# Turning the attention probabilities of 64-query halves by identity products on 64x64 parts, masking the first block like the others, and stepping chunk 2's mixing differently

## The chip, the core and the metric

The kernel runs on one core of a Trainium2 chip. The metric is the device time of one execution in microseconds (us); the kernel before is given by the median of three runs. The engines are TensorE (PE in the profile, its weight loads PEld), VectorE (DVE), ScalarE (ACT), GpSimd (POOL) and SyncE (SP), which issues most transfers (DMA).

## The reference, cut to what matters

One layer of a decoder trunk runs over 1,024 prompt tokens and 64 sample tokens: a SwiGLU block, a mixing layer, and a second SwiGLU block, each with a norm ahead and behind. The change lies in one half of the mixing layer, the sliding-window attention of the prompt. Eight query heads of 64 numbers share two key heads, a query sees the 128 positions before it and itself, and each head has a learned sink that takes part in the softmax's denominator:

```python
dist = qi + W - kj
band = (dist >= 0) & (dist <= WINDOW)
valid = (jnp.arange(nb)[:, None, None] > 0) | (kj >= W)[None]
s = jnp.where(band & valid, s, -jnp.inf)
m = jnp.maximum(jnp.max(s, -1, keepdims=True), sink)
p = jnp.exp(s - m)
p = p / (p.sum(-1, keepdims=True) + jnp.exp(sink - m))
out = jnp.einsum('bnhgqk,bnkhd->bnqhgd', p, vv)
```

The other half of the layer is a gated linear recurrence (HGRN2) in chunks. Everything is in float32.

## The kernel before, in words

**Chunks.** The 1,088 tokens are cut into three chunks: chunk 0 has 256 prompt tokens and the 64 sample tokens (320 wide), chunks 1 and 2 have 384 prompt tokens each. Nearly all the time goes to projections, in which each float32 operand is split into a rounded part and a remainder, and a product is made of three matmuls (lines 255 to 257, `mm3`). A weight tile comes by DMA (`raw`), ACT rounds it (line 235), DVE forms the remainder (line 236), and PE multiplies.

**Mixing beside projections.** What is not a projection is written as Python generators that stop at `yield`. A generator is registered as a stream with a rate. `tick()`, called once or twice for each weight tile, advances every stream by its rate, so mixing steps are dropped between projection products. `need(name)` runs the rest of a stream at once. The mixing streams are m0, m1 and m2, one for each chunk, with the rates `RM`. m0 runs beside the last part of the first SwiGLU block, m1 beside the output projection of chunk 0 and the input projection of chunk 2, m2 beside the output projection of chunk 1 and the first units of the second SwiGLU block (`f2.head`, whose cuts are `HEAD2`). In a mixing stream the recurrence (`intra`, then `hgrn_block`) and the attention (`attn_block`) take steps in turn. The framework then places each instruction on its engine by a planned timeline, so the order on an engine isn't quite that of the code. Each engine works its list in order.

**One attention block.** `attn_block(n, b)` works on 128 queries of chunk n, and does its eight heads in two rounds (`pr`) of four: two key heads `g`, two query heads `i`. A round has these steps:

- Scores, `sc`, line 1212: the 128 queries are two halves `hq` of 64. Each half needs 192 keys only, so the products are 64 queries by 192 keys, and the halves lie on the two halves of the partitions.
- Mask and maximum on DVE (line 1225), two tiny operations on the maxima (`sm`, lines 1228 and 1230), then the exponentials on ACT (line 1235), which write probabilities into the padded tile `pad` (512 wide, two heads of 192 with 64 columns at either end). POOL clears two corners of the pads (lines 1220 and 1221).
- After two yields the turning, `pT`, line 1248: PE's transpose takes windows of 64 queries by 128 keys and turns them, 16 of them in a round; a window may take in columns that are not wanted. One copy by DVE (`hq` 0) and one by ACT (`hq` 1) brings the turned tiles from PSUM to SBUF, 128x512 each (line 1253).
- After one more yield the product with the values, `pv`, line 1262: 12 products, each on 64 keys and 64 output columns, that take the four quarters of the PE array by turns. `PLACE` tells in which slot a half's key block `blk` stands. ACT and DVE copy and add the result (lines 1271 and 1272).

**The first block** of the prompt has no keys before it. There `cols_of` cuts the keys to 64 for the first half and 128 for the second, and mask and exponentials are done apart for each half: 8 of each in a round where other blocks have 4.

Names that the prediction uses besides: `lv` and `l` (lines 1316 and 1347) are products of the recurrence's `intra`; `av` (1403, 1406) those of its blocks; `pvT` (1280) the transposes of the attention's result; `tr` (452) transposes of the next SwiGLU block's or projection's input, for which line 444 scales rows by the root of `rsqrt`; `gb` (392) is a gain row that a DMA brings; `rb` (290) is a mean over partitions; `ar` is a piece of the SwiGLU activations that a DMA brings (993), rounded as `h`; `w` and `wsp` are weight tiles.

Of the kernel before, what the change touches and what calls it, by code (L numbers as in the profile page):

```python
# [8 lines left out]
F32 = mybir.dt.float32  # L9
# [4 lines left out]
AF = mybir.ActivationFunctionType  # L14
ALU = mybir.AluOpType
# [3 lines left out]
P = 128  # L19
# [11 lines left out]
NEG = -1e30  # L31
# [7 lines left out]
LEVELS = [64, 32, 16, 8, 4, 2, 1]  # L39
NRAW = 3  # L40
WARM = 12
PLACE = ((0, 0, 1), (1, 0, 0))
P1 = 1.0


# [1 line left out]
def tile_step(ctx: ExitStack, tc: tile.TileContext, A: dict, O: list):  # L47
    nc = tc.nc
    V, S, G, PE = nc.vector, nc.scalar, nc.gpsimd, nc.tensor
# [15 lines left out]
    def axbank(s="ax"):  # L65
        return ps.tile([P, 512], F32, tag="ax", bufs=4, name=uid(s))
# [53 lines left out]
    ident = cp.tile([P, P], F32, name="ident")  # L120
# [9 lines left out]
    halfpost = cp.tile([P, 16], F32, name="halfpost")  # L130
    sinkb = cp.tile([P, 8], F32, name="sinkb")
    amask = cp.tile([P, 192], F32, name="amask")
    smask = cp.tile([P, 136], F32, name="smask")
    ssink = cp.tile([P, 2], F32, name="ssink")
    seqm = cp.tile([NS, 4], F32, name="seqm")
# [10 lines left out]
    def mix_consts():  # L146
# [927 lines left out]
    def mixing(tp, h):  # L1074
        w_in, w_out = A["w_in"], A["w_out"][0]

        def t2(shape=(P, 512)):
            return tmp2("t2", shape)
# [21 lines left out]
        def w_in_units(n):  # L1100
# [88 lines left out]
        def attn_block(n, b):  # L1189
            zq, kx, vn = Z[n]["q"], KX[n], VN[n]  # L1190
            first = n == 0 and b == 0
            sm, mx = small(), small()
            of_ = t2()
            halves = (0, 1)

            def of(x, pr):
                return x.rearrange("p (g r i) -> p g r i", g=2, r=2)[:, :, pr]

            def cols_of(hq):
                return slice((128, 64)[hq] if first else 0, 192)  # L1200

            def rows(par):
                return slice(64 * par, 64 * par + 64)

            for pr in range(2):
                pt, banks = [], [axbank("sc")[:, :384].rearrange("p (i c) -> p i c", i=2) for _ in range(2)]
                for i in range(2):
                    for hq in halves:
                        cs = cols_of(hq)
                        k0 = b * P + 64 * hq  # L1210
                        for g in range(2):
                            PE.matmul(banks[g][rows(hq), i, cs],  # L1212
                                      zq[rows(g), 2 * pr + i, b * P + 64 * hq:b * P + 64 * hq + 64],
                                      kx[rows(g), k0 + cs.start:k0 + cs.stop], start=True, stop=True)
                parts = [(rows(hq), cols_of(hq)) for hq in halves] if first else [(slice(0, P), slice(0, 192))]
                for g in range(2):
                    pad = t2()
                    p = pad[:, 64:448].rearrange("p (i c) -> p i c", i=2)
                    pt.append((p, pad))
                    G.memset(pad[rows(0), 448:], 0.0)  # L1220
                    G.memset(pad[rows(1), :64], 0.0)
                    for i in range(2):
                        hd = 4 * g + 2 * pr + i
                        for rs, cs in parts:
                            V.tensor_tensor_reduce(out=p[rs, i, cs], in0=banks[g][rs, i, cs], in1=amask[rs, cs],
                                                   op0=ALU.add, op1=ALU.max, scale=1.0, scalar=NEG,
                                                   accum_out=mx[rs, 0, hd:hd + 1])
                V.scalar_tensor_tensor(of(sm[:, 0], pr), of(mx[:, 0], pr), 0.125, of(sinkb, pr),
                                       op0=ALU.mult, op1=ALU.max)
                V.tensor_scalar(of(sm[:, 1], pr), of(sm[:, 0], pr), -1.0, None, op0=ALU.mult)  # L1230
                for g in range(2):
                    for i in range(2):
                        hd = 4 * g + 2 * pr + i
                        for rs, cs in parts:
                            S.activation(pt[g][0][rs, i, cs], pt[g][0][rs, i, cs], AF.Exp, bias=sm[rs, 1, hd:hd + 1],  # L1235
                                         scale=0.125, accum_out=mx[rs, 1, hd:hd + 1])
                V.tensor_tensor(of(sm[:, 2], pr), of(sinkb, pr), of(sm[:, 0], pr), op=ALU.subtract)
                S.activation(of(sm[:, 2], pr), of(sm[:, 2], pr), AF.Exp)
                yield
                yield  # L1240
                pT, tb2 = [], [axbank("pT").rearrange("p (g i s q) -> p g i s q", g=2, i=2, s=2) for _ in range(2)]
                for g in range(2):
                    for i in range(2):
                        for slot, at in ((0, (0, 64)), (1, (128, -64))):
                            for hq in halves:
                                if not first or at[hq] >= cols_of(hq).start:
                                    c = 64 + 192 * i + at[hq]
                                    PE.transpose(tb2[hq][:, g, i, slot], pt[g][1][rows(hq), c:c + P],  # L1248
                                                 ident[rows(hq), rows(hq)])
                for hq in halves:  # L1250
                    t = t2((P, 2, 2, 2, 64))
                    ss = slice(1 - hq, 2 - hq) if first else slice(0, 2)
                    (S.copy if hq else V.tensor_copy)(t[:, :, :, ss], tb2[hq][:, :, :, ss])
# [3 lines left out]
                for turn in (((0, 0), (0, 1)), ((0, 2), (1, 0)), ((1, 1), (1, 2))):  # L1257
                    for g in range(2):
                        for par, (hq, blk) in enumerate(turn):
                            if 64 * blk >= cols_of(hq).start:  # L1260
                                alone = (hq, blk) in ((0, 1), (1, 1))
                                PE.matmul(ob[par][rows(g), :, hq], vn[rows(par), b + (blk + hq) // 2, rows(g)],  # L1262
                                          pT[hq][rows(par), g, :, PLACE[hq][blk]],
                                          start=alone or first or blk == 0, stop=alone or blk == 2)
                src = of_[:, pr * 256:pr * 256 + 256].rearrange("p (i h q) -> p i h q", i=2, h=2)
                if first:
                    S.copy(src[:, :, 0], ob[0][:, :, 0])
                    V.tensor_copy(src[:, :, 1], ob[0][:, :, 1])
                    V.tensor_tensor(src[:, :, 1], ob[1][:, :, 1], src[:, :, 1], op=ALU.add)
                else:  # L1270
                    S.copy(src, ob[0])
                    V.tensor_tensor(src, ob[1], src, op=ALU.add)
                if pr:
                    yield
            V.tensor_tensor(mx[:, 2], mx[:, 1], sm[:, 2], op=ALU.add)
            V.reciprocal(mx[:, 3], mx[:, 2])
            yield
            tb = axbank("pvT")
            for m in range(4):
                PE.transpose(tb[:, m * P:(m + 1) * P], of_[:, m * P:(m + 1) * P], ident)  # L1280
# [103 lines left out]
        def hgrn_block(n, b):  # L1384
# [458 lines left out]
```

## Time and profile before

| | |
|---|---|
| median of 3 runs | 1968.94 us (1964.67 to 1969.4) |
| the profiled execution: time, span | 1969.12 us, 1967.4 us |
| granted TensorE clock, mean | 0.996 |
| PE busy | 1942.1 us, 99% of the span |
| DVE busy | 1433.7 us, 73% |
| ACT busy | 949.6 us, 48% |
| POOL busy | 182.7 us, 9% |
| DMA, share of 16 engines on the hardware queue q1 | 54.4% |

Times in the profile are microseconds from the start of the span unless they are marked ns. A row of the timeline gives start, duration, engine, line, operation, the tiles written and read, the shape, and in square brackets the idle time before it and who ended that. `x24` is the number of records; a float32 product leaves two records (and two weight loads), a transpose or a product of rounded operands one. Such a row's duration goes from the first record's start to the last one's end. PEclk is the clock that the throttle granted to TensorE as a share of full speed.

### The profile page before, as it was taken

Reading aid. Unit: us, or ns where it says so; the run is one execution under the profiler, and the core shown is the slowest. Engines: PE = TensorE matmul, PEld = TensorE weight load, DVE = VectorE, ACT = ScalarE, POOL = GpSimd, SP = SyncE. Lnnn points to the kernel's source line nnn. Section 1 sums busy time; section 2 is a strip of 40 time slices with the busy share of each in tenths; the row PEclk is TensorE's granted clock in tenths of the full one; section 3 lists DMA queues with packets and bytes.
Section 4 is the critical chain, followed back from the end, with each engine's and each line's share of the span. In section 5 each row is a group of like instructions: output and inputs, shape, how many; then the busy total and the mean of one; then the engine's idle time right before and its main releaser. Section 6 shows DMA issues by size and latency. Waiting matters only on the chain.

```text
span 1967.4 us, 34910 instructions
## 1 busy us (share of the span) xinstructions
PE 1942.1 (99%) x13559; PEld 1817.4 (92%) x13559; DVE 1433.7 (73%) x2507; ACT 949.6 (48%) x1713; POOL 182.7 (9%) x225
## 2 busy tenths in 40 slices
PE   9999999999999999999999999999999999999998
PEld 9999999999998987778998898989999999999887
DVE  6896779886567646677577857866987877656666
ACT  5553445444445444445444545765544444445453
POOL 0300000000013102121031303000000000000202
PEclk9999999999999999999999999999999999999999
DMA  6643667655767546755434343536465545666974
GB/s 245 209 141 122 218 215 262 236 193 185 236 224 237 177 132 213 267 168 175 131 101 140 99 155 110 167 125 225 165 212 185 207 177 195 213 235 224 310 260 140
DMA packets 175606, 375.30 MB, mean 191 GB/s; under 512 B 16128, under 2 KB 67520, under 8 KB 175424
## 3 DMA queue, kind: packets, MB, share of 16 engines
q1 hardware_dynamic: 169536, 362.58, 54.4%
q10 hardware_dynamic: 5904, 10.49, 1.6%
q8 instruction: 106, 1.74, 0.3%
q14 instruction: 60, 0.49, 0.1%
HBM read 290.60 MB, written 83.39 MB: 190 GB/s over the span
## 4 chain that ended last, share of the span: by engine, by line
PE 88%; DMA 4%; DVE 4%; ACT 2%; issue 1%; POOL 0%; SPq 0%; ACTq 0%; DVEq 0%; POOLq 0%
PE mm L255 27%; PE mm L256 27%; PE mm L257 27%; DMA ar<-fa 1%; DMA raw<-in_ffn_w_gu_dram 1%; PE sc L1212 1%; ACT t L1235 1%; PE lv L1316 1%; DMA fb<-big 0%; PE pv L1262 0%; PE c L255 0%; PE c L257 0%; PE c L256 0%; DMA fa<-big 0%; PE pT L1248 0%
## 5 line engine op out<-in xcount | busy, mean ns | idle before, releaser
L255 PE MATMUL mm<-h,wsph 128*128 128x320 f32 (+1 forms) x1344 | 428.0, 319 | 0.0
L256 PE MATMUL mm<-h,wsph 128*128 128x320 f32 (+1 forms) x1344 | 425.2, 317 | 0.0
L257 PE MATMUL mm<-h,wspl 128*128 128x320 f32 (+1 forms) x1344 | 423.8, 317 | 0.0
L236 DVE TENSOR_TENSOR wspl<-raw,wsph 128x1024 fp32r<-128x1024 f32 x208 | 260.1, 1252 | 123.9 <-ACT wsph L235 123.1
L235 ACT CAST wsph<-raw 128x1024 fp32r<-128x1024 f32 x208 | 217.7, 1048 | 262.1 <-PE mm L256 211.0
L255 PEld LDWEIGHTS mm<-h,wsph 128*128 128x128 f32 x1344 | 252.8, 188 | 5.5 <-issue 3.8
L256 PEld LDWEIGHTS mm<-h,wsph 128*128 128x128 f32 x1344 | 252.9, 188 | 4.8 <-issue 4.0
L257 PEld LDWEIGHTS mm<-h,wspl 128*128 128x128 f32 x1344 | 252.4, 188 | 2.4 <-issue 2.1
L255 PE MATMUL mm<-h,w 128*128 128x384 f32 (+1 forms) x736 | 246.2, 334 | 3.0 <-ACT big L806 1.6
L256 PE MATMUL mm<-h,w 128*128 128x384 f32 (+1 forms) x736 | 245.5, 334 | 0.4 <-DVE h L617 0.3
L235 ACT CAST w<-raw 128x512 fp32r<-128x512 f32 (+1 forms) x208 | 153.5, 745 | 188.9 <-PE mm L256 93.5
L257 PE MATMUL mm<-h,w 128*128 128x384 f32 (+1 forms) x736 | 240.3, 333 | 0.5 <-POOL w L608 0.5
L236 DVE TENSOR_TENSOR w<-raw,w 128x512 fp32r<-128x512 f32 (+1 forms) x208 | 178.0, 862 | 75.6 <-ACT w L235 75.0
L256 PE MATMUL mm<-w,h 128*128 128x512 f32 x462 | 182.3, 395 | 0.9 <-DVE w L236 0.9
L255 PE MATMUL mm<-w,h 128*128 128x512 f32 x462 | 181.8, 396 | 0.7 <-DVE big L1006 0.7
L257 PE MATMUL mm<-w,h 128*128 128x512 f32 x462 | 180.8, 394 | 0.0
L256 PE MATMUL mm<-big,w 128*128 128x384 f32 x528 | 176.4, 334 | 0.0
L255 PE MATMUL mm<-big,w 128*128 128x384 f32 x528 | 176.4, 334 | 0.0
L257 PE MATMUL mm<-big,w 128*128 128x384 f32 x528 | 175.6, 334 | 0.0
L255 PEld LDWEIGHTS mm<-h,w 128*128 128x128 f32 x736 | 138.2, 188 | 4.8 <-ACT big L806 2.3
L256 PEld LDWEIGHTS mm<-h,w 128*128 128x128 f32 x736 | 138.2, 188 | 1.0 <-DVE h L617 0.8
L257 PEld LDWEIGHTS mm<-h,w 128*128 128x128 f32 x736 | 137.7, 188 | 1.1 <-POOL w L608 0.7
(346 smaller groups left out, 3379.8 us busy)
## 6 DMA issues: line engine op xcount, KB each, us to landing
raw<-in_ffn_w_gu_dram SPq DMA_DIRECT2D x162, 512.0 KB
raw<-in_ffn_w_down_dram SPq DMA_DIRECT2D x74, 512.0 KB
raw<-in_w_in_dram SPq DMA_DIRECT2D x54, 512.0 KB
ar<-fa SPq DMA_DIRECT2D x70, 384.0 KB
big<-in_ffn_w_down_dram SPq DMA_DIRECT2D x88, 256.0 KB
fb<-big SPq DMA_DIRECT2D x44, 512.0 KB
fa<-big SPq DMA_DIRECT2D x22, 768.0 KB
raw<-fb SPq DMA_DIRECT2D x30, 512.0 KB
```

What stands on the lines that cost most here:

```text
L235: made['S'] = S.copy(hi, src).ins
L236: (lo_eng or V).tensor_tensor(lo, src, hi.bitcast(F32), op=ALU.subtract)
L255: PE.matmul(out, a[0], b[0], start=first, stop=False, skip_group_check=resume)
L256: PE.matmul(out, a[0], b[1], start=False, stop=False, skip_group_check=resume)
L257: return PE.matmul(out, a[1], b[0], start=False, stop=last, skip_group_check=resume).ins
L1212: PE.matmul(banks[g][rows(hq), i, cs], zq[rows(g), 2 * pr + i, b * P + 64 * hq:b * P + 64 * hq + 64], kx[rows(g), k0 + cs.start:k0 + cs.st ...
L1235: S.activation(pt[g][0][rs, i, cs], pt[g][0][rs, i, cs], AF.Exp, bias=sm[rs, 1, hd:hd + 1], scale=0.125, accum_out=mx[rs, 1, hd:hd + 1])
L1316: PE.matmul(b5[32 * i:32 * i + 32, b, a], K[:, a, cs], Q[:, a, cs], start=True, stop=True)
```

## The change

The probabilities stand in a plain tile of 128 by 2 by 192. They are turned by 24 ordinary float32 products in a round, each of a 64x64 part with a 64x64 identity, where there were 16 transposes of 64x128 windows. Each part goes to the partitions on which the values' 64 rows stand, so a turned half fills one slot and half of another, and is copied in two pieces. The corners need no clearing. The first block uses the same 128 columns for both halves with a mask of its own (`amask1`), so mask and exponentials are done for all 128 partitions together. In chunk 2 there is one more yield ahead of `pv`; in chunks 1 and 2 one more ahead of a chunk's first `av`. The rates of m1 and m2 go from 0.92 and 1.2 to 1.08 and 1.30, and the first cut of `HEAD2` from 5 units to 4.

```diff
-PLACE = ((0, 0, 1), (1, 0, 0))
+TURNS = ((0, 0), (0, 1)), ((0, 2), (1, 0)), ((1, 1), (1, 2))
...
+        V.tensor_copy(amask1, amask[:, 64:192])
+        V.memset(amask1[0:64, 0:64], NEG)
...
-            if n:
+            if n == 0:
+                G.memset(kx[:, 64:P], 0.0)
+            else:
...
+            cs = slice(64 if first else 0, 192)
+            mask = amask1 if first else amask
+            pieces = [t for t in ((0, 0), (0, 1), (1, 1), (1, 0), (0, 2), (1, 2)) if not first or sum(t) > 1]
...
                 for g in range(2):
-                    pad = t2()
-                    p = pad[:, 64:448].rearrange("p (i c) -> p i c", i=2)
-                    pt.append((p, pad))
-                    G.memset(pad[rows(0), 448:], 0.0)
-                    G.memset(pad[rows(1), :64], 0.0)
+                    p = t2((P, 2, 192))
+                    pt.append(p)
                     for i in range(2):
                         hd = 4 * g + 2 * pr + i
-                        for rs, cs in parts:
-                            V.tensor_tensor_reduce(out=p[rs, i, cs], in0=banks[g][rs, i, cs], in1=amask[rs, cs],
...
+                        V.tensor_tensor_reduce(out=p[:, i, cs], in0=banks[g][:, i, cs], in1=mask,
...
-                        for rs, cs in parts:
-                            S.activation(pt[g][0][rs, i, cs], pt[g][0][rs, i, cs], AF.Exp, bias=sm[rs, 1, hd:hd + 1],
...
+                        S.activation(pt[g][:, i, cs], pt[g][:, i, cs], AF.Exp, bias=sm[:, 1, hd:hd + 1],
...
-                for g in range(2):
-                    for i in range(2):
-                        for slot, at in ((0, (0, 64)), (1, (128, -64))):
-                            for hq in halves:
-                                if not first or at[hq] >= cols_of(hq).start:
-                                    c = 64 + 192 * i + at[hq]
-                                    PE.transpose(tb2[hq][:, g, i, slot], pt[g][1][rows(hq), c:c + P],
-                                                 ident[rows(hq), rows(hq)])
+                for i in range(2):
+                    for g in range(2):
+                        for hq, blk in pieces:
+                            PE.matmul(tb2[hq][rows((hq + blk) % 2), g, i, blk // 2],
+                                      pt[g][rows(hq), i, 64 * blk:64 * blk + 64],
+                                      ident[rows(hq), rows(hq)], start=True, stop=True)
                 for hq in halves:
                     t = t2((P, 2, 2, 2, 64))
-                    ss = slice(1 - hq, 2 - hq) if first else slice(0, 2)
-                    (S.copy if hq else V.tensor_copy)(t[:, :, :, ss], tb2[hq][:, :, :, ss])
+                    copy = S.copy if hq else V.tensor_copy
...
+                        copy(t[:, :, :, 0], tb2[hq][:, :, :, 0])
+                        copy(t[rows(hq), :, :, 1], tb2[hq][rows(hq), :, :, 1])
                     pT.append(t)
                 yield
+                if n == 2:
+                    yield
...
             if b == 0:
                 yield
+                if n:
+                    yield
...
-    RM = [0.97, 0.92, 1.2]
+    RM = [0.97, 1.08, 1.30]
...
-    HEAD1, HEAD2 = 9, (5, 14, 22)
+    HEAD1, HEAD2 = 9, (4, 14, 22)
```

Because the timeline is planned anew, the order on the engines moves at many places of the mixing. Lines of the changed kernel lie some three to seven higher in number. Three places matter below. In the rows, numbers behind a name tell tiles of one kind apart, and only those within one kernel can be compared.

The first is DVE in the second round of the prompt's first block (chunk 0). Before, the last of the round's masked scores (the third and fourth of four 64-row operations on `t_1092`, the second bank) stand behind other work, and the tiny operations on the maxima (`sm_7301`), for which the exponentials wait, come after two operations of the recurrence (1331, 1355):

```order
L1225 ISA t_1092_7609,sm_7302<-sc_7593,amask 64x128
L1225 ISA sm_7302 64x1
L1331 COPY_PREDICATED cm_7214<-lm_88,lv_7628 128x256
L1355 TENSOR_TENSOR big_6792<-big_6792,big_7211 128x4x16x8
L1228 SCALAR_TENSOR_TENSOR sm_7301<-sm_7302,sinkb 128x2x2
L1230 TENSOR_SCALAR sm_7301<-sm_7301 128x2x2
L1237 TENSOR_TENSOR sm_7301<-sinkb,sm_7301 128x2x2
L236 TENSOR_TENSOR w_7853<-raw_7850,w_7852 128x1024
```

In the changed kernel:

```order
L1224 ISA t_1092_7602,sm_7306<-sc_7590,amask_84 128x128
L1224 ISA sm_7306 128x1
L1274 TENSOR_TENSOR t_1060_7307<-pv_7579,t_1060_7307 128x2x64
L1009 TENSOR_TENSOR big_6079<-mm_7179,big_6079 128x512
L1227 SCALAR_TENSOR_TENSOR sm_7305<-sm_7306,sinkb 128x2x2
L1009 TENSOR_TENSOR big_6079<-mm_7180,big_6079 128x512
L1229 TENSOR_SCALAR sm_7305<-sm_7305 128x2x2
L1235 TENSOR_TENSOR sm_7305<-sinkb,sm_7305 128x2x2
L239 TENSOR_TENSOR w_7790<-raw_7787,w_7789 128x1024
L1009 TENSOR_TENSOR big_6079<-mm_7181,big_6079 128x512
L239 TENSOR_TENSOR h_7961<-ar_7962,h_7961 128x2x384
```

The masks of the second bank and the three operations on the maxima now come ahead of the remainder of `w` (7790 is the same tile as 7800 before), behind which the second bank's masks stood, and ahead of the remainder of `h` (7961, before 7971). The recurrence's two operations (1336, 1360 in the new numbers) follow four rows further on.

The second is DVE where it makes the input of the second SwiGLU block's first transposes (`tr`, 452, read `big_5798`, which 444 writes). Before:

```order
L1272 TENSOR_TENSOR t_1159_8051<-pv_8440,t_1159_8051 128x256
L1380 TENSOR_TENSOR t_1230_8493<-hT_8488,big_7025 128x512
L224 SCALAR_TENSOR_TENSOR sm_8364<-sm_8364 128x3
L404 TENSOR_TENSOR big_7174<-big_7174,gb_8458 128x512
L1502 COPY t_1236_8539<-skT_8534 64x512
L1511 TENSOR_TENSOR t_1240_8546<-big_6922,seqm 64x512
L444 TENSOR_SCALAR big_5798<-big_5798,sm_8364 128x512 x3
```

In the changed kernel:

```order
L226 SCALAR_TENSOR_TENSOR sm_8356<-sm_8356 128x3
L1277 TENSOR_TENSOR t_1159_8041<-pv_8442,t_1159_8041 128x256
L227 SCALAR_TENSOR_TENSOR sm_8356<-sm_8356 128x3
L447 TENSOR_SCALAR big_5801<-big_5801,sm_8356 128x512 x2
L1385 TENSOR_TENSOR t_1230_8495<-hT_8490,big_7029 128x512
L447 TENSOR_SCALAR big_5801<-big_5801,sm_8356 128x512
L1174 TENSOR_TENSOR h_7214<-t_1230_8495,h_7212 128x4x128
L1509 COPY t_1236_8541<-skT_8536 64x512
L1518 TENSOR_TENSOR t_1240_8548<-big_6926,seqm 64x512
```

Two of the three scalings now stand ahead of the recurrence's operation (1380 before, 1385 now), and all three ahead of the sample tokens' (1502 and 1511, now 1509 and 1518).

The third is PE in the last round of chunk 0's attention, from the scores `sc` to the `pT` of the same round, for which mask, maxima and exponentials must be done in between. Before, 20 projection products of 512 columns stand there, beside the recurrence's eight `av` and four `u`:

```order
L1212 MATMUL sc_8225<-kx_6453,big_6520 64x192
L255 MATMUL mm_8410<-w_8311,h_8319 128x512
L256 MATMUL mm_8410<-w_8312,h_8319 128x512
L257 MATMUL mm_8410<-w_8311,h_8319 128x512
...
L1403 MATMUL av_8267<-big_6922,big_7212 128x128
L1406 MATMUL av_8267<-st,big_6792 128x128
...
L1410 MATMUL u_8339<-big_6922,t_1180_8178 128x128 x4
L256 MATMUL mm_8411<-w_8312,h_8319 128x512
...
L1248 MATMUL pT_8386<-ident,t_1189_8234 128x64
```

In the changed kernel ten do, and the `pT` follows right behind `u`:

```order
L1216 MATMUL sc_8221<-kx_6456,big_6524 64x192
L258 MATMUL mm_8011<-w_8177,h_8274 128x512
L259 MATMUL mm_8011<-w_8178,h_8274 128x512
L260 MATMUL mm_8011<-w_8177,h_8274 128x512
...
L1410 MATMUL av_8259<-big_6926,big_7216 128x128
L1413 MATMUL av_8259<-st,big_6796 128x128
...
L1417 MATMUL u_8331<-big_6926,t_1180_8174 128x128 x4
L1243 MATMUL pT_8378<-ident,t_1189_8230 64x64 x2
```

So the ten products that stood last between them have gone elsewhere. The same holds in the second round of chunk 1's second block, where 26 products of 384 columns, `av` and `u` lay between `sc` and `pT`, and now 15, `av` and four transposes (`kT`) do. Between `pT` and `pv`, under which the copies of the turned tiles run, there are at the end of chunk 2 twelve projection products in the last round and four in the round before it, where there were six and 25; in the other rounds nineteen instructions or more stand there before and after.

More of the change, by code (lines that the diff above doesn't have):

```diff
@@ L132, in tile_step @@
     amask = cp.tile([P, 192], F32, name="amask")
+    amask1 = cp.tile([P, P], F32, name="amask1")
     smask = cp.tile([P, 136], F32, name="smask")
@@ L1208, in attn_block @@
                     for hq in halves:
-                        cs = cols_of(hq)
                         k0 = b * P + 64 * hq
@@ L1214, in attn_block @@
                                       kx[rows(g), k0 + cs.start:k0 + cs.stop], start=True, stop=True)
-                parts = [(rows(hq), cols_of(hq)) for hq in halves] if first else [(slice(0, P), slice(0, 192))]
                 for g in range(2):
-                    pad = t2()
-                    p = pad[:, 64:448].rearrange("p (i c) -> p i c", i=2)
-                    pt.append((p, pad))
-                    G.memset(pad[rows(0), 448:], 0.0)
-                    G.memset(pad[rows(1), :64], 0.0)
+                    p = t2((P, 2, 192))
+                    pt.append(p)
                     for i in range(2):
                         hd = 4 * g + 2 * pr + i
-                        for rs, cs in parts:
-                            V.tensor_tensor_reduce(out=p[rs, i, cs], in0=banks[g][rs, i, cs], in1=amask[rs, cs],
-                                                   op0=ALU.add, op1=ALU.max, scale=1.0, scalar=NEG,
-                                                   accum_out=mx[rs, 0, hd:hd + 1])
+                        V.tensor_tensor_reduce(out=p[:, i, cs], in0=banks[g][:, i, cs], in1=mask,
+                                               op0=ALU.add, op1=ALU.max, scale=1.0, scalar=NEG,
+                                               accum_out=mx[:, 0, hd:hd + 1])
                 V.scalar_tensor_tensor(of(sm[:, 0], pr), of(mx[:, 0], pr), 0.125, of(sinkb, pr),
@@ L1250, in attn_block @@
                 for hq in halves:
                     t = t2((P, 2, 2, 2, 64))
-                    ss = slice(1 - hq, 2 - hq) if first else slice(0, 2)
-                    (S.copy if hq else V.tensor_copy)(t[:, :, :, ss], tb2[hq][:, :, :, ss])
+                    copy = S.copy if hq else V.tensor_copy
+                    if first:
+                        rs = rows(0) if hq == 0 else rows(1)
+                        copy(t[rs, :, :, 1], tb2[hq][rs, :, :, 1])
+                        if hq:
+                            copy(t[rows(0), :, :, 0], tb2[hq][rows(0), :, :, 0])
+                    else:
+                        copy(t[:, :, :, 0], tb2[hq][:, :, :, 0])
+                        copy(t[rows(hq), :, :, 1], tb2[hq][rows(hq), :, :, 1])
@@ L1254, in attn_block @@
                     pT.append(t)
                 yield
+                if n == 2:
+                    yield
                 ob = [axbank("pv")[:, :256].rearrange("p (i h q) -> p i h q", i=2, h=2) for _ in range(2)]
-                for turn in (((0, 0), (0, 1)), ((0, 2), (1, 0)), ((1, 1), (1, 2))):
+                for turn in TURNS:
                     for g in range(2):
                         for par, (hq, blk) in enumerate(turn):
-                            if 64 * blk >= cols_of(hq).start:
+                            if (hq, blk) in pieces:
```

6 lines of the change are left out of this document (2 added, 4 removed).

## The prediction

> **What bounds the kernel now.** First the span with its clock, then the page's busy times, the windows over the stretches that hold the mixing, and PE's waits in them.
>
> ```profile
> core 0: 1967.4 us, clock 0.996
> PE 1942.1 (99%) x13559; PEld 1817.4 (92%) x13559; DVE 1433.7 (73%) x2507; ACT 949.6 (48%) x1713; POOL 182.7 (9%) x225
> 720.00:850.00 130.00, 124.08 (x1172) 96.98 (x1171) 84.95 (x222) 59.08 (x151) 26.11 (x32) 0.96 0.64 213
> 1000.00:1150.00 150.00, 147.19 (x1280) 136.55 (x1268) 113.79 (x243) 75.86 (x161) 33.56 (x52) 1.00 0.37 118
> 1150.00:1320.00 170.00, 166.38 (x1780) 149.74 (x1779) 115.22 (x262) 100.87 (x213) 19.77 (x32) 1.00 0.44 145
> ```
>
> PE works 99% of the span: whatever is added to its list lengthens the run, and only PE's idle time or a withheld clock can be won back. A window's columns are its length, busy time of PE, PEld, DVE, ACT and POOL, granted clock, DMA share and GB/s. In the three windows PE idles 5.9 + 2.8 + 3.6 = 12.3 us. Most of it stands in few waits:
>
> ```profile
> PE tr L452 <- DVE big L444: 2.8, 1, 2.8
> PE pT L1248 <- ACT t L1235: 2.6, 6, 0.7
> PE rb L290 <- DVE ss L306: 2.1, 1, 2.1
> PE pv L1262 <- DVE t L1253: 1.7, 2, 1.4
> PE av L1406 <- DVE big L1355: 1.5, 1, 1.5
> ...
> PE pvT L1280 <- DVE t L1272: 0.6, 1, 0.6
> ```
>
> (Total, times, longest.) So the change is priced as PE time added, against these waits kept, gone or replaced.
>
> **The turning.** Rows of the timeline, and the tile `pT`:
>
> ```profile
> 984.22 0.71 PE L1248 MATMUL pT<-ident,t 64*128 64x64 f32 x16
> 989.53 0.89 PE L1262 MATMUL pv<-t,vn 64*64 64x128 f32 x24
> 1059.70 0.83 PE L1212 MATMUL sc<-kx,big 64*64 64x192 f32 x16
> 993.65 1.03 PE L1316 MATMUL lv<-big,big 128*32 128x32 f32 x96
> 776.22 1.15 PE L1347 MATMUL l<-big,big 128*64 128x64 f32 x16
> 737.91 0.46 PE L1248 MATMUL pT<-ident,t 64*128 64x64 f32 x8
> L1248 PE MATMUL pT<-ident,t x240: 222/223/273, 737.9 to 1307.7; 64*128 64x64 f32 x120
> L1253 ACT COPY t<-pT x16: 356/584/590, 740.4 to 1308.4; 128x512 f32<-128x512 f32 x14, 128x256 f32<-128x256 f32 x2
> L1253 DVE COPY t<-pT x16: 409/682/693, 742.1 to 1309.7; 128x512 f32<-128x512 f32 x14, 128x256 f32<-128x256 f32 x2
> ```
>
> A transpose left one record, a float32 product two (12 products of `pv`, x24). The 24 new products are 48 passes of 64 columns, 3072 in all, as `pv` (24 x 128) and `sc` (16 x 192) have. Their parts fill the array's quarters unevenly: 16, 8, 8 and 16 passes, so the heaviest quarter streams 1024 columns where one of `pv` streams 768. Off `pv`'s .89 I take the .22 that a single record lasts; the .67 left, times 4/3, is .89, so 1.11 a round: +.40 on .71. In fourteen full rounds that is +5.6. The first block's two rounds have 24 passes, 8 in each of three quarters: .67 x 512/768 + .22 = .67 against .46, +.4 for both. Turning: **+6.0**. The lower end is the cost of `pv` itself, +.18 a round, with the first block's some +2.7. The upper end is passes that don't overlap at all: by the `l` row a pass of 64 columns over the whole array takes (1.15 - .22)/15 = .062, 48 of them 3.0, so +2.3 in fourteen rounds and +1.0 in two, +34. I take 6.0, nearest to `pv`, which has the same quarters. The copies in two pieces cost by the shortest of their rows .41 x 2 on DVE and .36 x 2 on ACT, +.13 a round each; they count only where `pv` waits (below).
>
> The Trainium skill ("TensorE: Matmul & The Clock Gate", Part 3, "The mechanism") says that a weight load overlaps running matmuls only when its row group differs; here all loads of one half share theirs, and the sum would be higher (a rival below). The trace disagrees so far: `lv`, with 96 loads on the same 128 rows, took 1.03 us for the same 3072 columns.
>
> **The first block.** Its second round, by the timelines of DVE, ACT and PE and the clock after it:
>
> ```profile
> 752.62 1.87 DVE L236 TENSOR_TENSOR w<-raw,w 128x1024 fp32r<-128x1024 f32 x1
> 753.75 0.84 ACT L235 CAST h<-ar 128x768 fp32r<-128x768 f32 x1 [1.68 <-DMA ar<-fa]
> 758.21 0.16 DVE L1237 TENSOR_TENSOR sm<-sinkb,sm 128x4 f32<-128x4 f32 x1
> 758.39 0.35 ACT L1235 ACTIVATE t<-t,sm 64x64 f32<-64x64 f32 x1 [2.86 <-DVE sm L1237]
> 759.39 0.27 PE L1248 MATMUL pT<-ident,t 64*128 64x64 f32 x2 [0.20 <-ACT t L1235]
> 762.29 0.28 PE L1248 MATMUL pT<-ident,t 64*128 64x64 f32 x2 [0.69 <-ACT t L1235]
> 762.00:770.00 8.00, 7.71 (x28) 6.08 (x28) 4.06 (x8) 2.78 (x7) 2.72 (x4) 0.79 0.60 195
> ```
>
> `pT` stretches from 759.2 to 762.5 in four pieces, because eight exponentials run only from 758.39 on: 3.3 us for work of .46, a loss of 2.8, and then the clock is granted at .79 for 8 us, 1.7 more. By the first pair of order rows the new masks and maxima come ahead of the remainder that starts at 752.62; half as many exponentials start behind the cast of 753.75, at about 754.6, last some 2 us, and end before 757, two ahead of `pT`. The wait and its clock: **-4.5**. The first round holds the rest of the row of 2.6 (2.3 stand in this one): **-0.4**. POOL's clearing of corners goes at nothing: POOL is at 9%, and no wait names it.
>
> **The start of the second SwiGLU block.**
>
> ```profile
> 830.84 0.43 DVE L392 TENSOR_SCALAR gb<-gb 128x512 f32<-128x512 f32 x1 [4.03 <-DMA gb<-in_norm_ffn_post_dram]
> 832.92 1.23 DVE L236 TENSOR_TENSOR wspl<-raw,wsph 128x1024 fp32r<-128x1024 f32 x1
> 836.34 0.68 DVE L1502 COPY t<-skT 64x512 f32<-64x512 f32 x1
> 837.54 2.92 DVE L444 TENSOR_SCALAR big<-big,sm 128x512 f32<-128x512 f32 x3
> 839.81 1.81 PE L452 MATMUL tr<-ident,big 128*128 128x128 f32 x6 [2.83 <-DVE big L444]
> 840.00:848.00 8.00, 8.00 (x32) 6.05 (x32) 6.35 (x17) 3.59 (x7) 2.72 (x1) 0.65 0.27 92
> ```
>
> DVE is held by a transfer until 830.84, which the change doesn't touch, and then works off a list. In the new order the weight remainder (1.23) and the sample tokens' two operations (836.34 to 837.54, 1.2) no longer stand ahead of the scalings: some 2.5 sooner. PE comes some .9 sooner too, with four projection products of .23 fewer ahead of it: **-1.6**, and a wait of 1.2 is left. I leave the clock after it (8 x .35 = 2.8) as it is: ends 0 and -5.6 (wait and clock gone).
>
> **The other waits named.** `av` (1.5) has one more yield ahead of it in chunks 1 and 2: **-1.4**. `rb` is kept. At the end of chunk 2 the waits of `pv` (1.4) and `pvT` (.6) change with the products in front:
>
> ```profile
> 1222.72 0.49 PE L1406 MATMUL av<-st,big 128*128 128x128 f32 x2 [1.45 <-DVE big L1355]
> 1224.16 0.39 PE L1406 MATMUL av<-st,big 128*128 128x128 f32 x2
> 1299.68 0.83 PE L1212 MATMUL sc<-kx,big 64*64 64x192 f32 x16
> 1306.93 0.44 ACT L1235 ACTIVATE t<-t,sm 128x192 f32<-128x192 f32 x1
> 1308.54 0.31 PE L256 MATMUL mm<-h,wsph 128*128 128x320 f32 x1
> 1308.69 0.31 PE L257 MATMUL mm<-h,wspl 128*128 128x320 f32 x1
> 1080.00:1100.00 20.00, 20.00 (x119) 18.46 (x118) 18.28 (x34) 12.28 (x24) 4.34 (x5) 1.00 0.34 104
> ```
>
> At .15 each (the spacing of 1308.54 and 1308.69), 12 products give 1.8 us of cover in the last round and 4 give .6 in the one before it, against .9 now; I leave 1.3 of the 2.0: **-0.7**. **New waits**: the new order brings `pT` closer to `sc` at two places (the last order rows, and the place named behind them). In chunk 0's last round 10 products of 512 columns (.23, by width), `av` (eight in 1.8, by its two rows) and four of `u` like them lie between, about 5.0 us; in chunk 1's second block 15 of 384 (.17), `av` and four transposes, about 4.7. From the end of `sc` to the last exponential the round of 1299.68 took 6.9, with other work of DVE in between. By that the two wait 1.9 and 2.2, **+4.1** (before, ten and eleven projection products more covered them); with nothing in between they wait 0, and a queue like that of 1080 to 1100, where DVE worked 18.3 of 20 us, makes it more. I take the row. The moved unit of `HEAD2` is the same work later, and the few moves on SP's queue meet a DMA share of .37 to .44: 0.
>
> **Sum**: 6.0 - 4.5 - 0.4 - 1.6 - 1.4 - 0.7 + 4.1 = +1.5. The profiled execution took 1969.12 (span 1967.4 and 1.7 around it), .2 above the median of 1968.94: 1970.6 on its scale, 1970.5 on the median's.
>
> **Rivals.**
> - *Slower: the two new waits each bring a withheld clock.* A wait of 2.83 was followed by a clock of .65 (2.8 us lost); that of 2.06 at 1079 by 1.00. If DVE or ACT is one us further behind than in the row of 1299, both waits are 3.0 and each costs 2.8 behind it: 11.6 in place of 4.1, about 1978. It decides once a place costs 4.4. For it: DVE's 18.3 of 20. Against: the planner moved DVE's list too.
> - *Slower: loads not hidden.* By the `pT` row, two windows at a time, a window of 128 columns takes (.71 - .22)/8 = .061, one of 64 at most .03; 24 loads on each half add .72 a round, 10.1 in all: 1980.5. `lv`'s 1.03 speaks against it. This is the result of the skill's rule above.
> - *Slower: passes one after the other*: 34 in place of 6.0, about 1998. `pv` against.
> - *Faster: balanced turning and clean starts.* Turning at 2.7 (-3.3), `tr`'s wait and clock gone whole (-4.0), no new waits (-4.1). Two of the three give 1963, all three 1959. For it: the new order has DVE's scalings ahead.
>
> **How the numbers follow.** Within 0.3%, 5.9 us, a measurement of this kernel can hardly tell a change from none. The likeliest, about 1970.5 (own range 1965 to 1976), .44, of which .04 lies above that bound; the gated waits .27, loads .06, serial passes .04, faster .19. So faster .19, same .40, slower .41. The range 1959 to 1982 takes in the faster case, the gated waits and the loads; it leaves out the serial passes and the tails, under .15.
>
> **What would show it.** `pT` x48 in about 1.1 us (.89: balanced; 1.8: loads; 3.0: serial). No wait of `pT` on ACT in the first block, and a clock near 1 just behind it. A wait of `tr` near 1.2. `pT` waiting on ACT some 2 us in chunk 0's last round and chunk 1's second block, without a lower clock after. PE busy some 6 us more, less what the clock gives back. Wrong would be above all a clock withheld at a place that I don't name, or a wait of `pv` in many rounds.

## The result, and the profile after

The changed kernel's median is 1964.66 us over 20 runs (1960.4 to 1971.47), that of the kernel before 1967.36 over 20 (1962.64 to 1972.47). The ratio is 0.9988, with a 95% interval of 0.9979 to 0.9997: 2.4 us faster by the ratio, 2.7 by the medians, within the 0.3% that I had called hard to tell, and on the other side of the 1.5 us slower that I forecast. The time lies inside the range of 1959 to 1982, but .3 below the 1965 with which the likeliest case's own range began. (That range was counted from the 1968.94 of three runs; by the ratio, the change comes to 1966.6 on that scale, which is inside.) The direction is the faster rival's, to which I had given .19.

The profiled execution after took 1962.93 us, 1.7 below its median, as that of before was 1.8 above its own. So the two profiles differ by 6.2 us, 3.5 more than the medians, and what follows explains the profiles. First the cores' answer, the page's busy times, and the three windows of the mixing:

```profile
core 0: 1961.2 us, clock 0.998
PE 1945.0 (99%) x14039; PEld 1822.9 (93%) x14039; DVE 1440.6 (73%) x2507; ACT 949.9 (48%) x1713; POOL 169.0 (9%) x162
720.00:850.00 130.00, 127.65 (x1303) 101.16 (x1302) 90.42 (x213) 59.40 (x142) 21.35 (x20) 0.99 0.67 221
1000.00:1150.00 150.00, 150.00 (x1187) 140.22 (x1186) 111.06 (x244) 76.75 (x164) 24.00 (x26) 1.00 0.38 124
1150.00:1320.00 170.00, 169.06 (x2034) 151.06 (x2033) 118.06 (x267) 101.73 (x219) 17.05 (x12) 1.00 0.42 140
```

PE idles 2.4 + 0 + 0.9 = 3.3 us where it idled 12.3, and its busy time rose by 2.9 (1942.1 to 1945.0): 9.0 won and 2.9 lost are the 6 us between the profiles. PE's waits between 690 and 1330, and the rows of the turning:

```profile
PE pT L1243 <- ACT t L1233: 1.7, 2, 1.3
PE mm L258 <- ACT h L238: 0.5, 1, 0.5
PE oT L1187 <- DVE t L1182: 0.4, 1, 0.4
...
739.03 0.69 PE L1243 MATMUL pT<-ident,t 64*64 64x64 f32 x24
758.61 0.69 PE L1243 MATMUL pT<-ident,t 64*64 64x64 f32 x24
974.92 1.16 PE L1243 MATMUL pT<-ident,t 64*64 64x64 f32 x48
```

A full round's turning takes 1.16 us (.71 before), the first block's .69 (.46): 14 x .45 + 2 x .23 = 6.8 more. The five waits that I had listed (`tr`, `rb`, `pv`, `av`, `pvT`) are gone from the list, and of `pT`'s 2.6 us, 2.3 of them in the first block, nothing is left. The 1.7 that stand there are at another place, the first round of chunk 0's second block:

```profile
798.73 0.83 ACT L238 CAST h<-ar 128x768 fp32r<-128x768 f32 x1 [4.85 <-DMA ar<-fa]
800.06 0.46 PE L1243 MATMUL pT<-ident,t 64*64 64x64 f32 x12 [1.30 <-ACT t L1233]
758.00:766.00 8.00, 8.00 (x155) 6.46 (x156) 5.44 (x7) 3.43 (x7) 5.69 (x6) 1.00 0.65 209
800.00:808.00 8.00, 7.52 (x71) 6.31 (x72) 5.17 (x9) 4.00 (x13) 0.00 (x0) 0.79 0.60 200
826.08 0.43 DVE L395 TENSOR_SCALAR gb<-gb 128x512 f32<-128x512 f32 x1 [2.59 <-DMA gb<-in_norm_ffn_post_dram]
829.42 0.88 DVE L447 TENSOR_SCALAR big<-big,sm 128x512 f32<-128x512 f32 x2
835.21 1.20 PE L455 MATMUL tr<-ident,big 128*128 128x128 f32 x9
836.00:848.00 12.00, 11.41 (x54) 7.89 (x53) 8.37 (x15) 4.31 (x7) 1.90 (x2) 1.00 0.45 147
```

There ACT stood 4.85 us on a transfer of `ar` with the exponentials queued behind the cast, and the clock behind that wait is .79 for 8 us (1.7 lost). At the two old places it is 1.00: behind the first block's second round, and behind `tr`, which starts without a wait, 5 us after the first two scalings (447).

The two rounds in which I had put new waits of 1.9 and 2.2 us, from the end of `sc` to `pT`:

```profile
809.44 0.83 PE L1216 MATMUL sc<-kx,big 64*64 64x192 f32 x16
813.85 0.44 ACT L1233 ACTIVATE t<-t,sm 128x192 f32<-128x192 f32 x1
815.38 1.16 PE L1243 MATMUL pT<-ident,t 64*64 64x64 f32 x48
...
1050.27 0.87 PE L1216 MATMUL sc<-kx,big 64*64 64x192 f32 x8
1054.57 0.44 ACT L1233 ACTIVATE t<-t,sm 128x192 f32<-128x192 f32 x1
1056.06 1.16 PE L1243 MATMUL pT<-ident,t 64*64 64x64 f32 x48
```

The exponentials end 4.0 and 3.9 us after `sc`, not 6.9, and `pT` comes after 5.1 and 4.9 without a wait. The gaps (5.0 and 4.7 forecast) were right, the time of the chain in them was not.

### The profile page after: what moved, and what is told of

It is laid out like the page before. It is cut to its first block, busy times and chain, and to the rows that moved or that the text cites. A ratio compares the mean times of both kernels' runs of the same rounds, so it can differ in the third digit from the quotient of the medians.

```text
span 1961.2 us, 35769 instructions
## 1 busy us (share of the span) xinstructions
PE 1945.0 (99%) x14039; PEld 1822.9 (93%) x14039; DVE 1440.6 (73%) x2507; ACT 949.9 (48%) x1713; POOL 169.0 (9%) x162
## 4 chain that ended last, share of the span: by engine, by line
PE 89%; DMA 5%; DVE 3%; ACT 2%; issue 1%; POOL 0%; ACTq 0%; SPq 0%; DVEq 0%; POOLq 0%
PE mm L258 27%; PE mm L260 27%; PE mm L259 27%; DMA ar<-fa 1%; DMA raw<-in_ffn_w_gu_dram 1%; PE pT L1243 1%; PE lv L1321 1%; PE sc L1216 1%; DVE w L239 1%; DMA fa<-big 1%; PE pv L1267 1%; PE c L260 0%; PE c L258 0%; PE c L259 0%; DMA big<-in_ffn_w_gu_dram 0%
```

## The experiments

Write T for the turning, F for the first block's masks, O for the order (the two yields, the rates, the cut of `HEAD2`). In the rows, `hT` and `oT` are the transposes of the recurrence's and of the attention's result on their way to the output projection. Each ratio is to the kernel before, run on the same chip. Where a kernel is set beside the changed one or beside F alone, the two were run on different chips; the kernel before's medians there lay between 1967.0 and 1968.2, so such a difference is good to some 2 us, and the ratios are given where they say something else.

**T alone.** The pads go too, since only windows need them, and the turned halves are copied in two pieces:

```diff
-                                    PE.transpose(tb2[hq][:, g, i, slot], pt[g][1][rows(hq), c:c + P],
-                                                 ident[rows(hq), rows(hq)])
+                            PE.matmul(tb2[hq][rows((hq + blk) % 2), g, i, blk // 2],
+                                      pt[g][0][rows(hq), i, 64 * blk:64 * blk + 64],
+                                      ident[rows(hq), rows(hq)], start=True, stop=True)
```

> The kernel before with the new turning alone: 24 identity products, copies in two pieces, no pads to clear; masks, rates, yields and units as before. Theory A (the turning is PE time that nothing hides): pT x48 near 1.16 us as in the changed kernel, so +.45 in each of fourteen rounds and +.25 in two, about +6.8 us against the kernel before. Rival B (the order made anew decides, and PE's added time is given back by shorter waits): within 3 us of the kernel before.

Measured 1985.15 us, ratio 1.0092 (1.0075 to 1.0109): 17.8 us slower by the medians, beyond both theories. The profiles lie 14.7 us apart: PE's busy time rose by 5.2 us, the rest is idle time. The longest waits, 690 to 1340, and what held DVE ahead of the longest:

```profile
PE hT L1381 <- DVE sm L384: 5.1, 1, 5.1
PE mm L255 <- DVE big L1006: 4.3, 2, 3.6
PE rb L290 <- DVE ss L306: 3.5, 1, 3.5
...
835.21 0.43 DVE L392 TENSOR_SCALAR gb<-gb 128x512 f32<-128x512 f32 x1 [3.36 <-DMA gb<-in_norm_ffn_post_dram]
```

So the whole cost was more than twice the 6.8 us of the turning itself, because other waits stand on PE's list with it. This run doesn't separate what the newly made order does to them from what the copies in two pieces do (DVE is busy 4.7 us longer in all, ACT 4.4).

**F alone.**

```diff
+        V.tensor_copy(amask1, amask[:, 64:192])
+        V.memset(amask1[0:64, 0:64], NEG)
...
+            if n == 0:
+                G.memset(kx[:, 64:P], 0.0)
+            else:
...
-                        cs = cols_of(hq)
+                        cs = slice(64 if first else 0, 192)
...
-                parts = [(rows(hq), cols_of(hq)) for hq in halves] if first else [(slice(0, P), slice(0, 192))]
+                parts = [(slice(0, P), slice(64 if first else 0, 192))]
...
-                            V.tensor_tensor_reduce(out=p[rs, i, cs], in0=banks[g][rs, i, cs], in1=amask[rs, cs],
+                            V.tensor_tensor_reduce(out=p[rs, i, cs], in0=banks[g][rs, i, cs], in1=amask1 if first else amask,
```

> The kernel before with the first block masked like the others alone; turning by transposes, rates, yields and units as before. Theory A: the wait of pT on the exponentials in the first block's second round (2.3 us idle) and the withheld clock behind it (1.7 us) go, -4 to -5 us. Rival B: that wait is not there in most runs, or comes back at another place as the order is made anew: within 1.5 us of the kernel before.

Measured 1959.47 us, ratio 0.9961 (0.9948 to 0.9974): 7.9 us faster, the fastest of all kernels here that compute the layer, the changed one included. That is more than theory A's 4 to 5. Its waits and the scalings at the start of the second SwiGLU block:

```profile
PE rb L293 <- DVE ss L309: 2.1, 1, 2.1
PE pv L1267 <- DVE t L1258: 1.6, 2, 1.4
...
PE pT L1253 <- ACT t L1240: 0.3, 2, 0.2
...
828.62 0.88 DVE L447 TENSOR_SCALAR big<-big,sm 128x512 f32<-128x512 f32 x2
```

`pT`'s wait in the first block is gone, and so is `tr`'s 2.8: the scalings start at 828.62, not 837.54. So this second gain, which I had booked under the moved order, comes with the masks (and with the order that the planner makes for them). `rb`, `pv`, `av` and `pvT` wait as before.

**O alone.**

```diff
+                if n == 2:
+                    yield
...
+                if n:
+                    yield
...
-    RM = [0.97, 0.92, 1.2]
+    RM = [0.97, 1.08, 1.30]
-    HEAD1, HEAD2 = 9, (5, 14, 22)
+    HEAD1, HEAD2 = 9, (4, 14, 22)
```

> The kernel before with the two yields, the rates and the first unit of HEAD2 alone. Theory A: the waits of av (1.45), of tr (2.83, with 2.8 or more of withheld clock), of rb (2.06) and of pv at the end of chunk 2 (1.4) are a matter of the order and go: -4 to -9 us. Rival B: they stay, or others of the same size come: within 2 us of the kernel before.

Measured 1972.55 us, ratio 1.0024 (1.0013 to 1.0035): 5.2 us slower, outside both theories. `rb`, `av` and the long wait of `pv` are gone, as theory A had it, but `tr` keeps most of its wait and `oT` waits at the end of chunk 2, with a clock of .59 from 1310 to 1318 behind it:

```profile
PE oT L1182 <- DVE t L1177: 3.0, 1, 3.0
PE pT L1248 <- ACT t L1235: 2.9, 6, 0.7
PE tr L452 <- DVE big L444: 1.7, 1, 1.7
```

**T and F without O** (the changed kernel with the old yields, rates and cut).

> The changed kernel with the rates, the yields and the first unit of HEAD2 of the kernel before: new turning and new masks together. Theory A (parts add): +6.8 of the turning less 4 to 5 of the first block, +2 us against the kernel before. Rival B (the order decides): slower by 4 us or more, since the rates of before don't fit the new steps, or equal to the changed kernel, -2.5 us.

Measured 1971.3 us, ratio 1.0021 (1.001 to 1.0031): 4.0 slower than before, where rival B begins, though the interval of 2.0 to 6.1 nearly reaches theory A. The longest wait is that of the mean over partitions:

```profile
PE rb L293 <- DVE ss L309: 3.5, 1, 3.5
```

**F and O without T** (the changed kernel with transposes of padded windows).

> The changed kernel with the kernel before's turning (16 transposes of padded windows): new masks, yields, rates and unit. Theory A (each part has its own price): the changed kernel less its turning's +5.9 us of PE time, so some 1959. Rival B (yields, rates and unit suit the new turning only, as they cost 5 us on the kernel before): slower than the new masks alone (1959.5) by about 5, 1964 to 1965.

Measured 1965.87 us, ratio 0.9993 (0.9981 to 1.0005). Rival B: O costs F 5.5 us (-2.4 against -7.9), as it cost the kernel before 5.2, and with the same wait of `oT` (3.0).

**T and O without F.**

> The changed kernel with the kernel before's masks of the first block. Theory A: it loses what the masks gained on the kernel before, about 8 us, and comes to 1972 to 1973, with the wait of tr or of a neighbour at the start of the second SwiGLU block. Rival B: the 18 us that the new turning cost alone go back to the order, and the masks matter less once yields and rates are new: below 1968.

Measured 1977.25 us, ratio 1.0052 (1.0035 to 1.0068): 9.0 slower than before, 11.7 slower than with F, so theory A and more. `hT` waits 6.0 us for DVE at the end of chunk 0, as with T alone.

With these the eight combinations are complete (medians, us against the kernel before that was run beside each):

| | without T | with T |
|---|---|---|
| neither | 0 | +17.8 |
| F | -7.9 | +4.0 |
| O | +5.2 | +9.0 |
| F and O | -2.4 | -2.7 |

F gains in every row (7.6 to 13.8). O costs 5 to 6 with transposes and gains 7 to 9 with the identity products. T costs 18, 12 and 4, and beside F and O nothing that these medians tell apart. (Each entry's interval reaches 2 to 3 us to either side, so that the 4 is hardly clear.)

Why F gains in every row can be read in part at the end of chunk 0. In the profiles without F, PE waits there for DVE: `tr` 2.8 us before and 1.7 with O, `hT` 5.1 with T and 6.0 with T and O. With F neither waits there; the longest wait in its place is 1.5 (F and O). What holds DVE is a gain row's transfer (`gb`): DVE's operation on it starts at 828.6 to 836.5 in the four profiles without F and at 824.0 to 827.3 in the four with it.

**The kernel before again**, for a second profile.

> The kernel before again, for a second profile of it. If its waits are a matter of the order, tr, pT in the first block, rb, av and pv at the end of chunk 2 stand in it again, each within .5 us, and what differs lies elsewhere or in the clock behind them. If they are chance (transfers that came late once), some are missing.

```profile
PE tr L452 <- DVE big L444: 2.8, 1, 2.8
PE pT L1248 <- ACT t L1235: 2.6, 6, 0.7
PE rb L290 <- DVE ss L306: 2.1, 1, 2.1
PE pv L1262 <- DVE t L1253: 1.6, 2, 1.4
```

The named waits stand there again to a tenth of a us, and so does a lowered clock behind the first two (.79 from 762 to 770, and .71 from 840 to 848 where it was .65). They belong to the order, not to chance; the span was 1966.3, 1.1 less, and .7 of that lay before the mixing.

**Even quarters.**

```diff
-                            PE.matmul(tb2[hq][rows((hq + blk) % 2), g, i, blk // 2],
+                            PE.matmul(tb2[hq][rows((hq + blk + (0 if first else g)) % 2), g, i, blk // 2],
```

> The changed kernel with the parts of key head 1 turned onto the other half of the partitions, so that the four quarters of the array get 12, 12, 12 and 12 passes instead of 16, 8, 8 and 16; the second slot is copied in two pieces for each half, and the products with the values take those rows. The output is therefore not the layer's. If the heaviest quarter sets the time, a round's turning falls from 1.16 to about .9 us. If the loads of weights or the issue of 48 passes set it, it stays at 1.16.

```profile
971.31 0.98 PE L1243 MATMUL pT<-ident,t 64*64 64x64 f32 x48
```

.98 against 1.16, with the same 48 passes and loads: the heaviest quarter is a cause of the time, though only two thirds of the expected fall came. A limit by loads or issue alone is ruled out. (One run took 1956.72 us, with other waits too, so its time doesn't price the quarters.)

**O taken apart on the changed kernel.** Without the two yields:

> The changed kernel without the two new yields; rates and unit of HEAD2 as changed. If the rates carry what the new order wins back (rb's wait of 3.5 and its clock in the kernel with the old order are gone), it stays within 2.5 us of the changed kernel's 1964.7. If the yields do (room for the copies ahead of pv, and for the recurrence ahead of av), it goes towards 1971, with waits of pv or av above 1 us.

Measured 1974.68 us, ratio 1.0039 (1.0025 to 1.0053) to the kernel before, 10 above the changed kernel. The yields matter most, though not as I had it, `av` least of all:

```profile
PE oT L1187 <- DVE t L1182: 3.0, 1, 3.0
PE pT L1248 <- ACT t L1238: 2.2, 3, 1.7
PE pv L1270 <- DVE t L1260: 1.7, 1, 1.7
```

With the old rates:

> The changed kernel with the rates 0.92 and 1.2 of the kernel before; yields and unit as changed. If the rates carry it, rb waits about 3.5 us again with a withheld clock, and it comes to some 1971. If the yields do, it stays within 2.5 us of 1964.7, rb without a wait.

Measured 1968.07 us, ratio 0.9998 (0.9989 to 1.0007), 3.4 above the changed kernel by the medians and 2.0 by the ratios, and `rb` has no wait. So the rates don't carry it through `rb`; whether it stays within the 2.5 us of the second theory, these runs don't decide. What waits is the output projection of chunk 2, for the last block of the attention (`h` of 1173 and 1174, made from the result that `oT` turns). The longer of the two waits stands where DVE is held by a gain row's transfer once more, with the remainder of `h` behind it on its list:

```profile
PE mm L260 <- DVE h L1174: 2.5, 1, 2.5
PE mm L258 <- ACT h L1173: 1.7, 1, 1.7
...
1319.82 1.29 DVE L1613 TENSOR_TENSOR big<-big,gb 128x512 f32<-128x512 f32 x2 [2.27 <-DMA gb<-in_norm_mix_post_dram]
```

With `HEAD2` cut at 5:

> The changed kernel with the first cut of HEAD2 at 5 units as before; yields and rates as changed. The unit is the same PE work later, and I priced it at nothing: within 2 us of 1964.7. If it sets what covers the end of chunk 2, waits of oT, pv or u there add 3 us or more.

Measured 1972.22 us, ratio 1.0019 (1.0009 to 1.0029), 7.6 above the changed kernel (6.1 by the ratios). The waits for `h` are those two again (2.5 and 1.7), with the same transfer in DVE's way and a clock of .50 from 1322 to 1328: the unit that I had priced at nothing is not free. That it moves the point at which the projection asks for `h` is my reading; no run shows it apart from the new order.

F and the yield ahead of `av` alone:

> The kernel before with the new masks of the first block and, of the order's parts, the yield ahead of a chunk's first av alone. If that yield only removes the wait of av (1.4 us left with the masks alone), about 1958. If each new yield moves the planned order by as much as it wins, at or above the 1959.5 of the masks alone.

Measured 1964.25 us, ratio 0.9982 (0.9973 to 0.9991), 4.8 above F alone (4.1 by the ratios). The wait of `av` falls to .2, and the waits for `h` appear (2.6 and 1.7), again behind that transfer:

```profile
PE mm L260 <- DVE h L1174: 2.6, 1, 2.6
...
PE mm L258 <- ACT h L1173: 1.7, 1, 1.7
...
PE av L1410 <- DVE sm L1230: 0.2, 1, 0.2
```

**Is it one thing?** Three kernels keep an edit that brought such a wait and move chunk 2's rate alone: the last one at 1.24 (from 1.2), the one without yields at 1.24 (from 1.30), the one with the cut at 5 at 1.40 (from 1.30).

> New masks, old turning, the yield ahead of av, and chunk 2's rate at 1.24 in place of 1.2. Theory A (the place of chunk 2's last mixing steps against its output projection decides): the projection's waits for h (1.7 and 2.6 us, with a withheld clock) are gone with the rate a little higher, and it comes to 1958 to 1960. Rival B (any new order costs some us somewhere): at 1964 or above, with other waits.

> The changed kernel without the two new yields and with chunk 2's rate at 1.24 in place of 1.30. Theory A: without yields chunk 2's mixing runs too early against DVE, so oT waits 3.0 us and pv 1.7; a lower rate takes that back, to 1968 or below. Rival B: waits of the same size stay, 1972 or above.

> The changed kernel with HEAD2's first cut at 5 units and chunk 2's rate at 1.40 in place of 1.30. Theory A: with 5 units ahead the projection asks for h sooner than the mixing ends; a faster rate ends it in time, and the waits for h (1.7 and 2.5) go, to 1968 or below. Rival B: the waits stay or others come, 1971 or above.

Measured 1961.72, 1966.09 and 1973.41 us (ratios 0.9978, 0.9994 and 1.0032): 2.5 and 8.6 us better than before the rate was moved, and 1.2 worse. Only the second is clear of the noise: by the ratios the three differences are .8 and 8.9 better and 2.6 worse. In all three the wait that was aimed at is gone or small. In the first and the third a longer one stands in the list, of an ACT step (in the second, `lv` waits 1.9 us for DVE):

```profile
PE mm L258 <- ACT big L1606: 4.2, 1, 4.2
```

```profile
PE mm L258 <- ACT sg L714: 3.7, 1, 3.7
```

So theory A holds for the waits named. For the total it holds in the second, rival B in the third, and the first lies between them. What a new order leaves idle elsewhere stays unforeseen.

## Why the prediction was wrong

- **Turning, +6.0**: right in mechanism and nearly in size. 1.16 and .69 us a round where I had 1.11 and .67, +6.8 in all. The even quarters show that quarter load is a cause, and that the number of loads alone isn't what sets it, against the rival with loads that aren't hidden (1.8).
- **First block, -4.5**: right. Masks alone take `pT`'s wait from 2.6 to 0.3, and behind the second round the clock is 1.00. **-0.4**: misread. The rest of `pT`'s row stood not in the first round but between 1100 and 1120, in chunk 1. With masks alone it stays; that it is gone in the changed kernel was not foreseen.
- **`tr`, -1.6 with the clock left as it is**: mis-sized. The wait of 2.83 went whole and the clock behind it stayed at 1.00, some 4.0 us more, the far end that I had given. The scalings came 8 us sooner (829.4 against 837.5), not 2.5: the transfer that held DVE ended 4.8 sooner as well (DVE's `gb` operation at 830.84 before, at 826.08 after), which I had taken as untouched by the change. This is the step of the `tr` term that failed: the transfer is issued from ACT's list (rows below), so it moves with what stands ahead of it there, among it the exponentials of chunk 0's last round. These start at 819.73 before, after a wait of 5.66 for the maxima, and at 812.52 after, after one of 2.48.
- **`rb`, kept**: failed; its 2.1 us are gone. The wait stands in every profile without O (2.1 or 3.5) and in none that has any part of O, so it is the order's. **`av`, -1.4**: right. **End of chunk 2, -0.7**: all 2.0 went.
- **New waits, +4.1**: failed. I priced the chain from `sc` to the last exponential by one round of the old order in which DVE had other work in between (6.9); it took 4.0 and 3.9. The new wait came where I had none, at 800, behind a transfer on ACT's list, and cost 1.7 and 1.7 of clock.

```profile
824.70 0.34 ACTq L390 DMA_DIRECT2D gb<-in_norm_ffn_post_dram  x1
...
819.62 0.34 ACTq L393 DMA_DIRECT2D gb<-in_norm_ffn_post_dram  x1
```

(The issue before, and after.)

Put into the sum: +1.5 + 0.8 - 4.0 - 2.1 - 1.3 - 0.7 = -5.8, against -6.2 between the profiles. The medians lie 3.5 us nearer to each other, and no profile shows which part of this sum a median run holds. The steps that decided the sign are the waits that I kept from the old order, `tr`'s with its clock (4.0) and `rb`'s (2.1). That the term for new waits came out near is luck: 4.1 at two places fell away, and 3.4 came at a third. Of the rivals, the faster one had two of its three parts (`tr` clean, no waits at the two places), not the balanced turning, and for two parts it had given 1963; the gated waits did not come at the two places that it named.

## What to carry to other kernels

When a planner makes the order anew, the added PE time can be priced by itself, but not the waits; here it was 6.8 us, while the same edit moved the whole by 18, 12, 4 or 0, depending on what else was changed. Look for waits that stand near the end of a side stream, where the main work asks for its result: one yield, one unit, two yields or .06 of a rate moved the time by 4 to 10 us there. In several of these waits DVE was held by the transfer of a gain row, with the operation that PE needed behind it on its list: ask when such a transfer is issued, and from whose list. And measure an edit's parts: masking the first block like the others, alone, beats the whole change by 5 us.

## What the runs showed of the hardware that I had not expected

- Two profiles of one kernel agreed in each of the named waits to .1 us, while its run times spread over 10 (1962.64 to 1972.47): the idle time is in the order. The spread goes with the granted clock: of the 91 runs of the kernel before beside the experiments, 25 with a mean clock of .996 or less took 1970.2 us on average, 35 with .998 or more 1965.6.
- 48 passes of 64 columns took 1.16 us with quarters of 16, 8, 8 and 16, and .98 with 12 each: .045 for each pass that the heaviest quarter has less, below the .056 that `pv`'s row gives ((.89 - .22) / 12).
- The clock was withheld (.79 for 8 us) behind waits of 1.30 and .41 at 800, and granted in full behind one of 2.06 at 1079 in the kernel before. The length of a wait alone doesn't tell.
